# Row maxima of attention by two half-height matmuls, read as one pair of PSUM banks

## The chip, the cores and the metric

The kernel runs on one core of a Trainium2 chip. The core has five engines with queues of their own: TensorE (PE, with the weight load PEld beside it), VectorE (DVE), ScalarE (ACT), GpSimd (POOL) and SyncE (SP, which issues the DMAs). They meet through semaphores alone, and each starts its instructions in the order in which they stand in its queue. Matmul results go to PSUM, eight banks of 128 partitions x 512 float32. The metric is the device time of one execution in microseconds.

## The reference, cut to what matters

One encoder layer over 2048 tokens of width 1024. The input projection gives queries (8 heads of 64), keys and values (2 heads each) and 512 channels for a state-space model (SSM); two mixers run on them, and an output projection and a SwiGLU feed-forward follow.

```
s = einsum('bqgrd,bkgd->bgrqk', q_blk, k) * scale      # q, k: normalised and rotated
p = softmax(s, axis=-1)
o = einsum('bgrqk,bkgd->bqgrd', p, v)
```

The softmax needs no particular number as the maximum of a row: whatever is subtracted from the scores before the exponential falls out of the quotient again. It only has to lie near the true maximum.

## The kernel before

Inputs are float32. Where a product has to keep more digits than one matmul pass gives, an operand is held as a high part (rounded) and a low part (the rest).

The first stage (modulation, norm, input projection, L368) ends near 380 us. The second, 380 to 1340 us, is attention and the SSM. Attention is cut into 16 *units*: 4 blocks of 512 queries by 4 pairs of heads. For each unit `prep_q` turns the queries of two heads into operands: `qa[h]` holds the high part of head h's queries in one half of the 128 partitions and the low part in the other, `qb[h]` the high part once more and, in its second half, minus the row maxima. `ka[kv][f]` holds the high part of the keys in both halves. `prep_max` finds the maxima: for each of 4 groups of 512 keys, 2 heads and 4 blocks of 128 queries one matmul over all 128 partitions into one bank (L712, tile `ps_s1`, "ps_s" in the trace), and one VectorE maximum of it (L713, `mx`): 32 of each in a unit. The banks are `ps_1` (two) and `ps_2` (one), taken in turn. Then `m8` joins the four groups (L717), L719 turns the sign, and eight small matmuls (L723, `ps_mt`) bring the result into the rows of `qb`.

`unit` takes 16 steps of 128 keys. A step has, for each head, two matmuls into one of two `ps_st` banks (L784 with `qa` and `ka`, L785 with `qb` and `kb`, which adds minus the maximum) and an exponential on ScalarE (L787), and for both heads the product with the values (L770, `ps_o`): head 1 goes to columns 64 to 127 of TensorE's array and head 0 to columns 0 to 63, and each is two passes, since the operands are plain float32. The sums of the exponentials are on GpSimd and VectorE; `EM` says how often a step's goes to VectorE. `finish` normalises a unit (L736, L743, L749).

`advance` puts the preparation of later units between these steps, and `run(bg, 1)` the steps of the SSM: 8 chunks, with scans (L875, L876) and 1024-element products (L128, L854) on VectorE and more on GpSimd. The program order is only a priority: a scheduler with a timeline of its own decides the order in which instructions stand on each engine, and that order is fixed in the program. `tc.high_priority(KOFF)` lets the first unit's preparation come as early as its buffers allow.

Of the kernel before, what the change touches and what calls it, by code (L numbers as in the profile page):

```python
# [9 lines left out]
F32 = mybir.dt.float32  # L10
# [33 lines left out]
EM = 16  # L44
# [20 lines left out]
def tile_encoder(ctx: ExitStack, tc: tile.TileContext, I, O, stop=None, dbg=None):  # L65
# [37 lines left out]
    def rstd(pool, ss, n, width, tag):  # L103
        """(ss / width + eps) ** -0.5 on [P, n]"""
        t = pool.tile([P, n], F32, tag=tag + "a", name=tag + "a")
        GP.tensor_scalar(t, ss, 1.0 / width, EPS, op0=ALU.mult, op1=ALU.add)
        r = pool.tile([P, n], F32, tag=tag + "b", name=tag + "b")
        GP.tensor_tensor(r, t, mhalf[:, :n], op=ALU.pow)
        return r

    # ------------------------------------------------------------------ constants from parameters
# [20 lines left out]
    def cmul(ore, oim, are, aim, bre, bim, t0, t1, eng=V):  # L132
        """(ore, oim) = a * b; t0, t1 temporaries"""
# [7 lines left out]
    def rot_levels(rot, rt, lv, gs, n, eng):  # L141
        """doubles the length of the rotor tables of n groups"""
# [6 lines left out]
    with ExitStack() as p1:  # L149
# [15 lines left out]
        # ---- tables of the SSM  # L165
# [26 lines left out]
        def expand(ch, eng=V):  # L192
            """state-in, state-out and in-chunk tables of GC groups"""
# [16 lines left out]
            # re: cre*are - cim*aim; minus im: ncim*are - cre*aim  # L210
# [19 lines left out]
            # impulse responses within a chunk; columns: forward only | backward only | both  # L230
# [25 lines left out]
        # ---- conditioning vector and the columns of the small parameters  # L256
# [18 lines left out]
        def row_of(i):  # L275
            """selects row i of nr for all partitions"""
# [4 lines left out]
        def ada_chunk(c0, w, tag="ad"):  # L281
            """columns c0 to c0 + w of c_act @ w_ada"""
# [70 lines left out]
        def modulate(tf, src, ht, ks, eng):  # L353
            """hi and lo parts of the modulated rows, transposed"""
# [15 lines left out]
        def ssm_setup():  # L370
            # ---- SSM parameters
# [16 lines left out]
            # dt = exp(log_dt)  # L388
# [6 lines left out]
            # exp(lr * dt) - 1 through tanh  # L395
# [7 lines left out]
            # angle reduced to [-pi, pi]  # L403
# [30 lines left out]
            # powers 0..8  # L434
# [12 lines left out]
            # unit rotor of 8 steps (backward: conjugate) and its doublings, renormalised; decay of 8 steps  # L447
# [10 lines left out]
            # directional power tables  # L458
# [8 lines left out]
            # the state input is turned back by one chunk: pbd = pb0 * e^{-i phi}, where phi is 8 steps  # L467
            # in the direction of time; un holds e^{i phi} forward and its conjugate backward
# [7 lines left out]
        def ssm_setup2(kre, kim):  # L476
# [21 lines left out]
            # Bbar = k * b  # L498
# [7 lines left out]
        # the first tiles advance with the weights  # L506
# [20 lines left out]
        def in_main(s, ht, ta, begun):  # L527
# [8 lines left out]
            def norm_rope(src, i, n):  # L536
                """heads of src, rotated, and their reciprocal norms"""
# [50 lines left out]
        def rotors(chunks, eng, tags):  # L588
            """e^{i phi m} over the half chunks"""
# [35 lines left out]
    # ------------------------------------------------------------------ attention and SSM  # L625
# [5 lines left out]
    with ExitStack() as p2:  # L631
        ps_1 = p2.enter_context(tc.tile_pool(name="ps_1", bufs=2, space=PSUM, reuse_waits="tile"))
        ps_2 = p2.enter_context(tc.tile_pool(name="ps_2", bufs=1, space=PSUM, reuse_waits="tile"))
        ps_c = p2.enter_context(tc.tile_pool(name="ps_c", bufs=1, space=PSUM, reuse_waits="tile"))
        ps_m = p2.enter_context(tc.tile_pool(name="ps_m", bufs=1, space=PSUM, reuse_waits="tile"))
        ps_s = p2.enter_context(tc.tile_pool(name="ps_s", bufs=2, space=PSUM, reuse_waits="tile"))
# [7 lines left out]
        turn = cycle((ps_1, ps_1, ps_2))  # L644

        def scores(u, name):
            return (next(turn) if u else ps_1).tile([P, 512], F32, tag="s1", name=name)
# [14 lines left out]
        def prep_k(g, first):  # L662
            """keys as split parts: the high part of the first head, or the rest"""
            pt = scores(0, "ps_kt")
# [14 lines left out]
        def prep_q(u):  # L679
            """queries of a block for a pair of heads, as split parts"""  # L680
# [4 lines left out]
            pt = misc("ps_qt") if u else scores(u, "ps_qt")  # L685
# [9 lines left out]
            V.tensor_sub(qa[1][hi], pt[hi], qa[1][hi])  # L695
            A.copy(qa[1][lo], pt[hi])
            A.copy(qb[1][lo], qa[1][lo])
# [512 lines left out]
```

## Time and profile before

| | |
|---|---|
| median of 3 executions | 3050.98 us (3050.66 to 3051.86) |
| span of the profiled execution | 3050.2 us (the profile gives no other time of it) |
| busy PE, PEld | 2901.0 us (95%), 2129.6 us (70%) |
| busy DVE, ACT, POOL | 1598.9 us (52%), 1156.6 us (38%), 1279.9 us (42%) |
| maxima, TensorE (L712) | 512 matmuls, 211.6 us busy |
| maxima, VectorE (L713) | 512 reductions, 333.1 us busy, 682 ns each |

The span runs from the first instruction to the last. Busy shares are averages over stages that have different limits; PE's ends are modelled, so its busy time also covers gaps between close matmuls. What a change in the second stage is worth has to be read from that stage.

### The profile page before, as it was taken

The numbers are of one execution on the slowest core, as the hardware profiler recorded it, in microseconds if no ns is written. First come the engines' busy times: TensorE is split into PE (matmuls) and PEld (weight loads), VectorE is DVE, ScalarE is ACT, GpSimd is POOL, SyncE is SP. The second block draws the span as 40 slices with busy tenths as digits, with TensorE's granted clock in tenths as the row PEclk, the third lists the DMA queues.
The fourth block names the chain that finished last, engine by engine and source line by source line (L and its number), as shares of the span: only waits on it lengthen the run. The fifth ranks groups of instructions, "written<-read, shape, count | busy, mean of one in ns | idle before, by whom it ended". The sixth has DMA issues, their size and how long they took to land.

```text
span 3050.2 us, 36157 instructions
## 1 busy us (share of the span) xinstructions
PE 2901.0 (95%) x13548; PEld 2129.6 (70%) x13548; DVE 1598.9 (52%) x2271; ACT 1156.6 (38%) x2227; POOL 1279.9 (42%) x1062
## 2 busy tenths in 40 slices
PE   6998978889889999999999999999999999999998
PEld 4776835445445455458878888888888888888887
DVE  6879886777887755653343333433334332343323
ACT  3654544444444445452333222322223222232222
POOL 3647568778888977433231111211112111121112
PEclk7999998989999999999999999999999999999999
DMA  7764221111110100022254332533334332243322
GB/s 211 216 221 152 86 69 41 49 45 49 45 45 25 56 11 11 4 90 83 87 173 124 97 97 93 178 98 97 98 122 152 97 97 97 91 153 97 98 98 80
DMA packets 331648, 292.24 MB, mean 96 GB/s; under 512 B 44024, under 2 KB 278224, under 8 KB 330448
## 3 DMA queue, kind: packets, MB, share of 16 engines
q1 hardware_dynamic: 331472, 289.92, 30.0%
q8 instruction: 107, 1.75, 0.2%
q14 instruction: 69, 0.57, 0.1%
HBM read 243.24 MB, written 46.64 MB: 95 GB/s over the span
## 4 chain that ended last, share of the span: by engine, by line
PE 69%; DVE 4%; issue 1%; POOL 1%; ACT 1%; DVEq 0%; POOLq 0%; ACTq 0%
PE ps_h L1102 31%; PE ps_y L986 6%; PE ps_f L1134 5%; PE ps_f L1135 5%; PE ps_f L1136 5%; PE ps_o L770 4%; PE ps_st L784 2%; PE ps_s L712 2%; PE ps_st L785 2%; PE ps_z L986 2%; DVE xs L876 1%; DVE xs L875 1%; DVE mx L713 1%; DVE ys L128 1%; PE ps_t L977 1%
## 5 line engine op out<-in xcount | busy, mean ns | idle before, releaser
L1102 PE MATMUL ps_h<-ht,w_hi 128*128 128x512 f32 x2816 | 869.4, 390 | 2.3 <-DVE ht L1088 2.3
L1069 DVE TENSOR_TENSOR w_lo<-w_raw,w_hi 128x1024 fp32r<-128x1024 f32 x248 | 305.9, 1234 | 680.8 <-ACT w_hi L1068 680.6
L1068 ACT CAST w_hi<-w_raw 128x1024 fp32r<-128x1024 f32 x264 | 277.9, 1053 | 983.8 <-issue 628.8
L1102 PEld LDWEIGHTS ps_h<-ht,w_hi 128*128 128x128 f32 x2816 | 528.9, 188 | 112.2 <-DVE ht L1088 2.6
L1102 PE MATMUL ps_h<-ht,w_lo 128*128 128x512 f32 x1408 | 548.5, 390 | 0.4 <-DVE w_lo L1069 0.4
L1110 POOL TENSOR_TENSOR act<-th,act 128x512 fp32r<-128x512 f32 x88 | 157.1, 1786 | 775.9 <-ACT act L1109 775.9
L713 DVE TENSOR_REDUCE mx<-ps_s 128x1 f32<-128x512 f32 x512 | 333.1, 682 | 107.7 <-PE ps_s L712 105.6
L1102 PEld LDWEIGHTS ps_h<-ht,w_lo 128*128 128x128 f32 x1408 | 264.8, 188 | 55.8 <-DVE w_lo L1069 0.8
L1135 PE MATMUL ps_f<-w_hi,act 128*128 128x512 f32 x704 | 274.2, 389 | 0.0
L1136 PE MATMUL ps_f<-w_lo,act 128*128 128x512 f32 x704 | 273.9, 390 | 0.0
L1134 PE MATMUL ps_f<-w_hi,act 128*128 128x512 f32 x704 | 273.8, 390 | 0.0
L712 PE MATMUL ps_s<-ka,qa 128*128 128x512 f32 x512 | 211.6, 454 | 48.3 <-DVE mx L713 46.9
L368 PE MATMUL ps_z<-whi,ht 128*128 128x512 f32 (+1 forms) x768 | 226.9, 379 | 15.0 <-ACT ht L357 11.0
L784 PE MATMUL ps_st<-qa,ka 128*128 128x512 f32 x512 | 224.9, 439 | 14.9 <-ACT e__6941 L787 2.5
L712 PEld LDWEIGHTS ps_s<-ka,qa 128*128 128x128 f32 x512 | 93.6, 192 | 189.0 <-DVE mx L713 133.2
L785 PE MATMUL ps_st<-qb,kb 128*128 128x512 f32 x512 | 208.3, 407 | 0.1
L986 PE MATMUL ps_y<-wo,mt 128*128 128x512 f32 x768 | 186.2, 394 | 1.2 <-DVE on L751 0.9
L1108 DVE SCALAR_TENSOR_TENSOR th<-th,ps_h 128x512 f32<-128x512 f32 x88 | 60.5, 687 | 227.0 <-PE ps_h L1102 226.8
L368 PEld LDWEIGHTS ps_z<-whi,ht 128*128 128x128 f32 x768 | 141.1, 199 | 44.8 <-ACT ht L357 12.8
L784 PEld LDWEIGHTS ps_st<-qa,ka 128*128 128x128 f32 x512 | 98.9, 193 | 102.7 <-issue 21.7
L986 PEld LDWEIGHTS ps_y<-wo,mt 128*128 128x128 f32 x768 | 142.1, 188 | 35.3 <-DVE mt L980 4.7
L1135 PEld LDWEIGHTS ps_f<-w_hi,act 128*128 128x128 f32 x704 | 132.2, 188 | 27.3
(2266 smaller groups left out, 5041.5 us busy)
## 6 DMA issues: line engine op xcount, KB each, us to landing
w_raw<-in_w_ffn_in_dram SPq DMA_DIRECT2D x176, 512.0 KB
w_raw<-in_w_ffn_out_dram SPq DMA_DIRECT2D x88, 512.0 KB
wa<-in_w_ada_dram SPq DMA_DIRECT2D x48, 512.0 KB
xt<-in_x_dram SPq DMA_DIRECT2D x32, 512.0 KB
rot_d<-rot SPq DMA_DIRECT2D x16, 512.0 KB
rotl<-rot_d SPq DMA_DIRECT2D x8, 1024.0 KB
x_d<-xt SPq DMA_DIRECT2D x16, 512.0 KB
x2n<-x_d SPq DMA_DIRECT2D x16, 512.0 KB
```

What stands on the lines that cost most here:

```text
L368: T.matmul(pp[:, 0:c1 - c0], ht[:, a, k], w[:, k, c0:c1], start=k == 0 and j == 0, stop=k == KD - 1 and j == 2)
L712: T.matmul(p1_, qa[h][:, P * j:P * (j + 1)], ka[kv][f], start=True, stop=True)
L713: red = V.reduce_max(mx[:, 4 * h + j, f:f + 1], p1_, axis=AX.X)
L784: T.matmul(st_, ka[kv][k // 4][:, ks], qa[h], start=True, stop=False)
L785: T.matmul(st_, kb[kv][k // 4][:, ks], qb[h], start=False, stop=True)
L986: T.matmul(out, lhs[:, a, k], rhs[w][k][:, cs_], start=n == 0, stop=n == last)
L1068: A.copy(hi, raw)
L1069: (GP if cnt % 4 == 3 else V).tensor_sub(lo, raw, hi)
L1102: T.matmul(pp, w[:, k], ht[:, a, k], start=n == 0, stop=n == 23)
L1134: T.matmul(pf[j], act[0][:, f, js], hi[:, e], start=f == 0, stop=False)
L1135: T.matmul(pf[j], act[1][:, f, js], hi[:, e], start=False, stop=False)
L1136: T.matmul(pf[j], act[0][:, f, js], lo[:, e], start=False, stop=f == KF - 1)
```

## The change

The scores of which the maximum is taken are now made of the high parts of the queries alone, so they need only 64 partitions. Head 0's high part lies in partitions 0 to 63 and head 1's, by a changed `prep_q`, in 64 to 127 (which also saves one ScalarE copy in a unit). Two half-height matmuls (L714), one for each head, go to the two banks of one tile `pair`, and one VectorE reduction reads both (L720): 16 pairs and 16 reductions in a unit, each of twice the length. `pair` has one buffer of two banks where there were three of one; the bank left over goes to `ps_s`, which has three now, and the keys and the first unit's queries are transposed through these instead of through `ps_1`. In the first unit every second pair takes two of them too. `EM` goes from 16 to 8: in the first 13 units one more step of the 16 (the ninth) adds its two exponentials on VectorE and no longer on GpSimd.

```diff
-EM = 16
+EM = 8
-        ps_1 = ...tile_pool(name="ps_1", bufs=2, space=PSUM, ...)
-        ps_2 = ...tile_pool(name="ps_2", bufs=1, space=PSUM, ...)
+        ps_1 = ...tile_pool(name="ps_1", bufs=1, space=PSUM, ...)
-        ps_s = ...tile_pool(name="ps_s", bufs=2, space=PSUM, ...)
+        ps_s = ...tile_pool(name="ps_s", bufs=3, space=PSUM, ...)
...
-            pt = scores(0, "ps_kt")
+            pt = single("ps_kt")
...
-            V.tensor_sub(qa[1][hi], pt[hi], qa[1][hi])
-            A.copy(qa[1][lo], pt[hi])
-            A.copy(qb[1][lo], qa[1][lo])
+            V.tensor_sub(qa[1][lo], pt[hi], qa[1][hi])
+            A.copy(qb[1][lo], qa[1][hi])
...
-                for h in range(2):
-                    for j in range(4):
-                        p1_ = scores(u, "ps_s1")
-                        T.matmul(p1_, qa[h][:, P * j:P * (j + 1)], ka[kv][f], start=True, stop=True)
-                        red = V.reduce_max(mx[:, 4 * h + j, f:f + 1], p1_, axis=AX.X)
-                        yield
+                for j in range(4):
+                    js = slice(P * j, P * (j + 1))
+                    if u == 0 and j % 2:
+                        both = [single(f"ps_s{h}") for h in range(2)]
+                    else:
+                        pair = ps_1.tile([P, 2, 512], F32, tag="s1", name="ps_s1")
+                        both = [pair[:, h] for h in range(2)]
+                    for h, own in enumerate((lo, hi)):
+                        mm = T.matmul(both[h], qa[h][own, js], ka[kv][f][own], start=True, stop=True)
+                    tc.keep_in_program_order(mm)
+                    if u == 0 and j % 2:
+                        for h in range(2):
+                            red = V.reduce_max(mx[:, 4 * h + j, f:f + 1], both[h], axis=AX.X)
+                    else:
+                        red = V.reduce_max(mx[:, j::4, f], pair, axis=AX.X)
+                    yield
+                    yield
```

(`single` takes a bank of `ps_s`. The rest of the diff is comments. Lines after the maxima have numbers higher by 8: L784 is L792 now, L770 is L778, L723 is L731.)

The scheduler makes another order of it, and it differs in three ways.

First, the end of a unit on TensorE, here where the maxima of the twelfth unit become complete. Before, the last maxima stood singly between scores and value products (L770), and steps of the running unit followed them on both sides of `ps_mt`:

```order
L712 MATMUL ps_s1_9496<-ka13_4577,qa1_9265 128x512
L784 MATMUL ps_st_9930<-qa1_8784,ka12_4576 128x512
L785 MATMUL ps_st_9930<-qb1_8786,kb12_4586 128x512
L712 MATMUL ps_s1_9499<-ka13_4577,qa1_9265 128x512
L770 MATMUL ps_o_9621<-e__9919,v_sb_91 64x512
L770 MATMUL ps_o_9621<-e__9914,v_sb_91 64x512
L784 MATMUL ps_st_9939<-qa0_8783,ka13_4577 128x512
```

Now six pairs stand one behind the other at this place (the last three are shown), then the eight `ps_mt` matmuls, and then the scores of the next unit (L793), which need them:

```order
L714 MATMUL ps_s1_9093<-ka13_4574,qa0_8914 128x512
L714 MATMUL ps_s1_9093<-ka13_4574,qa1_8915 128x512
L714 MATMUL ps_s1_9097<-ka13_4574,qa0_8914 128x512
L714 MATMUL ps_s1_9097<-ka13_4574,qa1_8915 128x512
L714 MATMUL ps_s1_9115<-ka13_4574,qa0_8914 128x512
L714 MATMUL ps_s1_9115<-ka13_4574,qa1_8915 128x512
L731 MATMUL ps_mt_9122<-ident_60,mn1_4576 64x128 x4
L731 MATMUL ps_mt_9128<-ident_60,mn1_4576 64x128 x4
L793 MATMUL ps_st_9588<-qb0_8916,kb10_4581 128x512
L793 MATMUL ps_st_9622<-qb0_8916,kb10_4581 128x512
```

Ten pairs of each unit were moved into the unit's run and six behind its last value products; since `pair` has one buffer, each of the six waits for the reduction of the one ahead. This group of six stands at the end of every unit from the seventh on, and the earlier units have such groups of up to six, some with matmuls of the SSM between.

Second, the middle of a unit on TensorE. Before, a maximum's matmul stood among matmuls of its own shape, all over 128 partitions:

```order
L785 MATMUL ps_st_9895<-qb0_8785,kb12_4586 128x512
L712 MATMUL ps_s1_9453<-ka13_4577,qa0_9264 128x512
L784 MATMUL ps_st_9900<-qa1_8784,ka12_4576 128x512
L785 MATMUL ps_st_9900<-qb1_8786,kb12_4586 128x512
L770 MATMUL ps_o_9621<-e__9868,v_sb_91 64x512
```

Now a pair over 64 partitions each stands between two scores over 128:

```order
L793 MATMUL ps_st_9523<-qb0_8468,kb13_4584 128x512
L714 MATMUL ps_s1_9027<-ka11_4572,qa0_8914 128x512
L714 MATMUL ps_s1_9027<-ka11_4572,qa1_8915 128x512
L792 MATMUL ps_st_9528<-qa1_8467,ka13_4574 128x512
L793 MATMUL ps_st_9528<-qb1_8469,kb13_4584 128x512
L778 MATMUL ps_o_9238<-e__9517,v_sb_91 64x512
```

Some ten blocks of pairs in a unit stand like this, with another shape of matmul on both sides or on one.

Third, the SSM on TensorE. Its last output matmuls (`ps_y`, L895 before, L904 now) stood in the tenth unit before:

```order
L895 MATMUL ps_y_9217<-ckl_8748,ys_9035 128x128 x2
L896 MATMUL ps_y_9217<-tp_8750,ut_8804 128x128
L712 MATMUL ps_s1_8929<-ka11_4575,qa1_8784 128x512
L784 MATMUL ps_st_9378<-qa0_8304,ka01_4571 128x512
L785 MATMUL ps_st_9378<-qb0_8306,kb01_4581 128x512
```

Now they stand ahead of the maxima of the seventh unit, shortly before its `ps_mt`:

```order
L903 MATMUL ps_y_8867<-ckl_8431,ys_8687 128x128 x2
L904 MATMUL ps_y_8867<-tp_8433,ut_8484 128x128
L714 MATMUL ps_s1_6878<-ka13_4574,qa0_6662 128x512
L714 MATMUL ps_s1_6878<-ka13_4574,qa1_6663 128x512
L714 MATMUL ps_s1_6882<-ka13_4574,qa0_6662 128x512
```

So the eight chunks of the SSM lie beside six units instead of beside ten. At the start of the stage, the transposes of the keys and all maxima of the first unit stand behind the last projection matmul (L368) now; 24 of those 32 maxima stood between projection matmuls before.

## Rows read from the trace of the kernel before

**Rows 1.** Busy time in three stretches: us, PE, PEld, DVE, ACT, POOL, clock, DMA.

```profile
394.20:794.20 400.00, 343.42 (x1456) 188.00 (x1456) 306.70 (x324) 178.90 (x314) 330.22 (x222) 0.91 0.15 45
794.20:1054.70 260.50, 231.98 (x960) 125.84 (x961) 205.84 (x222) 117.52 (x209) 218.63 (x142) 0.92 0.14 40
1054.70:1284.30 229.60, 229.60 (x974) 117.03 (x972) 137.98 (x223) 119.92 (x208) 155.14 (x124) 1.00 0.03 10
```

**Rows 2.** Chain of work, 1067 to 1293 us, shares by line.

```profile
by line: PE ps_o L770 34.4%; PE ps_s L712 20.2%; PE ps_st L784 18.9%; PE ps_st L785 16.1%; PE ps_mt L723 4.0%; PE ps_rs L736 2.2%; PE ps_z L986 1.3%; PE ps_qt L687 1.0%; PE ps_ot L749 1.0%; PE ps_rt L743 0.9%; PE ps_t L977 0.2%
```

**Rows 3.** The same stretches, the maxima's reductions (L713) alone: VectorE busy, count.

```profile
394.20:794.20 400.00, 124.18 (x192) 0.91 0.15 45
794.20:1054.70 260.50, 82.84 (x128) 0.92 0.14 40
1054.70:1284.30 229.60, 104.71 (x160) 1.00 0.03 10
```

**Rows 4.** Timeline of TensorE in a late unit: start, duration, instruction.

```profile
1085.87 0.64 PE L770 MATMUL ps_o<-e__9816,v_sb 128*64 128x512 f32 x1
1085.87 0.64 PE L770 MATMUL ps_o<-e__9811,v_sb 128*64 128x512 f32 x1
...
1086.87 0.51 PE L712 MATMUL ps_s<-ka,qa 128*128 128x512 f32 x1
1087.22 0.40 PE L784 MATMUL ps_st<-qa,ka 128*128 128x512 f32 x1
```

**Rows 5.** Timeline of TensorE, a value product of one head alone.

```profile
628.98 1.07 PE L770 MATMUL ps_o<-e__6508,v_sb 128*64 128x512 f32 x2
629.98 0.50 PE L712 MATMUL ps_s<-ka,qa 128*128 128x512 f32 x1
```

**Rows 6.** Timeline of TensorE around matmuls over 64 partitions (L743, 64*128).

```profile
1069.36 0.40 PE L784 MATMUL ps_st<-qa,ka 128*128 128x512 f32 x1
1069.59 0.40 PE L785 MATMUL ps_st<-qb,kb 128*128 128x512 f32 x1
1069.92 0.46 PE L743 MATMUL ps_rt<-ident,acc 64*128 64x64 f32 x4
1070.31 0.51 PE L784 MATMUL ps_st<-qa,ka 128*128 128x512 f32 x1
1070.65 0.40 PE L785 MATMUL ps_st<-qb,kb 128*128 128x512 f32 x1
```

**Rows 7.** Timeline of VectorE in the same unit as Rows 4.

```profile
1077.23 0.69 DVE L713 TENSOR_REDUCE mx<-ps_s 128x1 f32<-128x512 f32 x1 [2.10 <-PE ps_s L712]
...
1087.42 2.08 DVE L713 TENSOR_REDUCE mx<-ps_s 128x1 f32<-128x512 f32 x3 [0.95 <-PE ps_s L712]
...
1097.81 0.19 DVE L717 TENSOR_REDUCE m<-mx 128x8 f32<-128x32 f32 x1
1098.03 0.18 DVE L719 TENSOR_SCALAR mn<-m 128x8 f32<-128x8 f32 x1
```

**Rows 8.** Timeline of TensorE where the first stage ends, the first unit's last maxima.

```profile
378.99 0.39 PE L368 MATMUL ps_z<-wlo,ht 128*128 128x512 f32 x1
...
382.04 1.10 PE L712 MATMUL ps_s<-ka,qa 128*128 128x512 f32 x2 [0.18 <-DVE mx L713]
383.32 1.10 PE L712 MATMUL ps_s<-ka,qa 128*128 128x512 f32 x2 [0.18 <-DVE mx L713]
```

**Rows 9.** Timeline of ScalarE, the first exponential.

```profile
394.16 0.60 ACT L787 ACTIVATE e__4804<-ps_st 128x512 f32<-128x512 f32 x1
```

**Rows 10.** Busy time while TensorE waited at a unit's end; columns as in Rows 1.

```profile
676.00:680.00 4.00, 0.91 (x3) 0.48 (x4) 3.97 (x2) 1.16 (x2) 4.00 (x3) 0.90 0.00 0
...
684.00:688.00 4.00, 2.67 (x7) 1.67 (x7) 3.94 (x7) 1.50 (x2) 3.73 (x6) 0.50 0.00 0
```

**Rows 11.** Two of the SSM's groups on VectorE: count, shortest/median/longest ns.

```profile
L128 DVE TENSOR_TENSOR ys<-st,st x32: 1206/2000/2364, 418.0 to 1016.6; 128x1024 f32<-128x1024 f32 x32
L875 DVE TENSOR_TENSOR_SCAN xs<-r,ys x16: 2269/3170/3371, 427.2 to 990.8; 64x1023 f32<-64x1023 f32 x16
```

More of the change, by code (lines that the diff above doesn't have):

```diff
@@ L631, in tile_encoder @@
     with ExitStack() as p2:
-        ps_1 = p2.enter_context(tc.tile_pool(name="ps_1", bufs=2, space=PSUM, reuse_waits="tile"))
-        ps_2 = p2.enter_context(tc.tile_pool(name="ps_2", bufs=1, space=PSUM, reuse_waits="tile"))
+        ps_1 = p2.enter_context(tc.tile_pool(name="ps_1", bufs=1, space=PSUM, reuse_waits="tile"))
         ps_c = p2.enter_context(tc.tile_pool(name="ps_c", bufs=1, space=PSUM, reuse_waits="tile"))
         ps_m = p2.enter_context(tc.tile_pool(name="ps_m", bufs=1, space=PSUM, reuse_waits="tile"))
-        ps_s = p2.enter_context(tc.tile_pool(name="ps_s", bufs=2, space=PSUM, reuse_waits="tile"))
+        ps_s = p2.enter_context(tc.tile_pool(name="ps_s", bufs=3, space=PSUM, reuse_waits="tile"))
         ps_o = p2.enter_context(tc.tile_pool(name="ps_o", bufs=1, space=PSUM, reuse_waits="tile"))
@@ L642, in tile_encoder, with single @@
         ab = p2.enter_context(tc.tile_pool(name="ab", bufs=3, reuse_waits="tile"))
-        turn = cycle((ps_1, ps_1, ps_2))
-        def scores(u, name):
-            return (next(turn) if u else ps_1).tile([P, 512], F32, tag="s1", name=name)
+        def single(name):
+            return ps_s.tile([P, 512], F32, tag="st", name=name)
         def misc(name, tag="am"):
@@ L684, in prep_q @@
             yield
-            pt = misc("ps_qt") if u else scores(u, "ps_qt")
+            pt = misc("ps_qt") if u else single("ps_qt")
             for j in range(4):
```

## The prediction

> **What bounds the kernel now.** I read the busy time by stretches first, because the change touches only the second stage. I cut this stage where `ps_mt` of the seventh, eleventh and sixteenth unit starts, so that the stretches hold the maxima of 6, 4 and 5 units, 192, 128 and 160 reductions [rows 3]. In the last stretch TensorE is busy all of its 229.6 us, the clock is 1.00 and VectorE has 138.0 us of work [rows 1]. The chain of waits there is nothing but TensorE's lines, and the maxima's matmuls are 20.2% of it [rows 2]. This stretch has no SSM. Work for the next stage (`ps_z` and `ps_t`) is 1.5% of the chain [rows 2], 3.4 us, so a unit takes (229.6 − 3.4) / 5 = 45.2 us.
>
> The two stretches before have the SSM beside the units, 400.0 us for six and 260.5 for four. There no engine is full: VectorE 306.7 / 400.0 = 77%, GpSimd 83%, and TensorE gets its clock for 0.91 to 0.92 on average [rows 1]. TensorE waits for reductions that stand behind the SSM's long instructions in VectorE's queue, and when it has waited long, the granted clock falls from 1.00 to 0.50, 1.2 GHz of the two levels [rows 10].
>
> **What the change is worth on TensorE alone.** A matmul of 512 columns costs 0.23 us from start to start [rows 6], so the 32 of a unit cost 7.4 us. Two matmuls in different parts of the array can run at once: the two heads' value products, in separate column halves, start in the same hundredth of a microsecond and take 1.00 us for both [rows 4], and one head alone takes the same 1.00 [rows 5]. No row shows two row halves at once. I take it that they overlap as the column halves do: 0.24 us for a pair instead of 0.47, with 0.47 as the other bound.
>
> The price is the change of shape. L743 works over 64 partitions: it starts 0.33 us after the matmul ahead, where 0.23 is usual, and the matmul behind it is followed after 0.34 [rows 6]. That is 0.10 + 0.11 = 0.21 for going in and out. It may be more, since the value product also has a long last pass ahead of the change; I take 0.30 for a block, between 0.21 and 0.40. So a lone pair costs 0.24 + 0.30 = 0.54, against 0.47 before: of the halving nothing is left. The Trainium skill (TensorEngine Tiling (Array Packing), Theoretical Speedup) gives up to twice the speed for a contraction of 64 rows or fewer; by that alone nine late units would save 9 x 16 x 0.23 = 33 us. The same page (Key Properties) says that another tiling mode drains TensorE, and with its 0.10 on either side the trace agrees with that. The sum goes by the rows.
>
> **The six pairs at a unit's end.** They are 12 matmuls in sequence on one buffer, so each waits for the reduction of the one ahead. From a maximum's matmul to its reduction pass 0.55 us (1086.87 [rows 4] to 1087.42 [rows 7]). The reduction over 1024 elements is not in the trace. It takes 0.69 us for 512 elements and 0.19 for 32 [rows 7], 1.04 ns an element, so 1.22 for 1024; the bounds are 0.69 (the second bank free) and 1.38 (twice one). I take 1.22. A waiting matmul starts some 0.03 us later, so the pitch is 0.55 + 1.22 + 0.03 = 1.8 us, and five waits take 9.0. The first unit of before shows the pattern with two buffers: two matmuls every 1.28 us, each group after a wait for a reduction [rows 8]. After the last pair follow 0.55 + 1.22, the joining (0.19) and the sign (0.18) [rows 7], with small gaps 2.2 us, until `ps_mt` starts. Before, all this lay beside value products and scores; now nothing else stands ahead of the next unit's scores on TensorE.
>
> **A late unit after the change**, then: 45.2 − 7.4 + 9 lone pairs at 0.24 (2.2) + one split pair (0.5) + ten changes of shape at 0.30 (3.0) + 9.0 + 2.2 = 54.7 us. During the six pairs TensorE works 0.24 of each 1.8 us, little like the stretch in which the clock fell [rows 10]; work at half speed around them I put at 1.3 us, between 0 and 4. That makes 56 us (53.5 to 60). Nine units look like this, since the SSM is through after six: 9 x 56 = 504 us for what took 260.5 + 229.6 = 490.1. **Term: +14 us.**
>
> **The first six units** now have all of the SSM. VectorE's work there, without maxima: 306.7 − 124.2 = 182.5 us, and from the second stretch 205.8 − 82.8 = 123.0, less four units' other work at the last stretch's (138.0 − 104.7) / 5 = 6.7, so 96 [rows 1, 3]. The maxima are 96 reductions, 117 us at 1.22 (they were 124.2); `EM` adds 12 sums of 0.69, 8 us (and takes as many from GpSimd, where they are worth nothing while it is not the last). Together 403 us. At the 77% of before this takes 523 us, without a gap 403. The denser packing should close some gaps, but each reduction has TensorE's 0.55 us ahead of it unless SSM work stands between; I take 84%, 480 us (430 to 540). **Term: 480 − 400 = +80 us.** TensorE stays just below that: 6 x 56 = 336 and, for the SSM, 343.4 + 232.0 − 10 x 45.2 = 123 [rows 1], 459 us, some of it in gaps between the pairs.
>
> **The start.** The last projection matmul is at 379.0 [rows 8] and the first exponential at 394.2 [rows 9], 15 us. Now the transposes, eight double and sixteen single reductions (8 x 1.22 + 16 x 0.64 = 20 us, 0.64 being half of 1.28 [rows 8]) and some 10 us ahead and behind stand in this gap, 30 us. The first stage gets rid of 24 maxima and 20 transposes, some 7 us. **Term: +8 us** (3 to 13).
>
> The third score bank and the saved ScalarE copy I cost at nothing: where units run without SSM, TensorE is never idle, so nothing waits for a score bank in the end. If the scores after `ps_mt` waited for ScalarE, the bank would save a part of a microsecond a unit. The last unit and the later stages have no maxima and stay.
>
> **Sum.** +8 + 80 + 14 = +102 us on a span of 3050.2, which stands 0.8 us below the median of the runs: **3153 us**.
>
> **Rivals.** *The row halves do not overlap*, so the change does not do what it says. Then a pair costs 0.23 us more; behind VectorE's work this is hidden, but in the nine late units 15 adjacent pairs each cost it: 9 x 15 x 0.23 = +31, **3184 us**. For it: no row shows two row halves at work. Against it: the column halves overlap fully [rows 4, 5]. The Trainium skill (TensorE: Matmul & The Clock Gate, Part 3) puts concurrent row tiles some 4 ns apart, which no row here can show.
>
> *The packed SSM pays for everything, and the kernel is faster.* Place: VectorE in the first six units. Its SSM instructions take 2.00 and 3.17 us in the median, but 1.21 and 2.27 at best [rows 11]. The stage has 64 of the 1024-element products and 32 scans, so at best prices 64 x 0.8 + 32 x 0.9 = 80 us less: 403 − 80 = 323, at 88% 367 us. With late units at 54.7 the sum is +8 − 33 + 2 = −23, **3028 us**. It decides once the six units take less than 400 − 8 − 14 = 378 us. For it: the trace has such instructions. Against it: GpSimd, whose work beside VectorE goes with the long ones, is 83% busy there [rows 1] and has more SSM per unit now.
>
> *The gaps stay as they were*: VectorE is no denser than 77%, and the clock falls in each group of six. 523 − 400 = 123, 9 x 59 − 490 = 41, with 8 **3222 us**. For it: the groups of maxima at the unit ends alternate with SSM work in one queue, and TensorE stalls there already.
>
> **How the numbers follow.** The forecast 0.66, gaps as before 0.14, halves in sequence 0.10, the faster case 0.07, and 0.03 for a sum that comes out at nothing. The range is 3080 to 3240. The forecast's terms at their bounds give 3 + 30 − 9 = +24 and 13 + 140 + 50 = +203; I cut both ends a little, since not all terms stand at one end together. The range holds the two slower rivals and leaves the faster case out. Within 0.2% (6 us, what a measurement here can tell from no change) is 0.02; faster 0.08, slower 0.90.
>
> **What would show it.** In the profile after, the late units' `ps_mt` should be 54 to 60 us apart, not 45, with six pairs 1.7 to 1.9 us apart ahead of each, TensorE waiting for L720; a reduction of 1.2 us; the second half of a pair within 0.02 us of the first; `ps_mt` of the seventh unit near 880 us instead of 794; the later stages shifted alone. It is wrong if the groups of six take under 5 us, or if the seventh unit's `ps_mt` comes before 790.

## The result, and the profile after

The changed kernel takes 3328.22 us (3325.25 to 3331.64, 4 runs), the kernel before 3050.82 us beside it: ratio 1.0913 (1.0897 to 1.0928). The prediction had 3153 us and a range of 3080 to 3240. The sign was right, the loss was 277 us instead of 102, well outside the range. The profiled execution has a span of 3329.9 us at a mean clock of 0.931.

I cut the stage at the first `ps_mt` matmul of the first, seventh, eleventh and last unit. In [rows 1] the first stretch began at the first exponential instead (394.2 us, now 431.3); the first `ps_mt` stood at 385.8 there. The windows view of the changed kernel (us, PE, PEld, DVE, ACT, POOL, clock, DMA) answers to [rows 1]:

```profile
423.70:979.40 555.70, 405.55 (x1680) 214.22 (x1680) 365.78 (x288) 199.84 (x349) 359.36 (x246) 0.83 0.15 42
979.40:1234.70 255.30, 211.86 (x769) 91.34 (x769) 101.84 (x111) 93.17 (x167) 129.35 (x105) 0.86 0.05 16
1234.70:1551.60 316.90, 263.97 (x965) 113.31 (x965) 135.97 (x150) 112.96 (x200) 136.99 (x110) 0.87 0.02 7
```

The last stretch matters most. Before, TensorE was busy in all of it at a clock of 1.00; now it has no SSM either, but TensorE is busy 264.0 of 316.9 us, at a clock of 0.87, and VectorE 43%. Neither engine is full. The groups on the profile page of the changed kernel (sums over the whole kernel) say why:

```profile
L720 DVE TENSOR_REDUCE mx<-ps_s 128x2 f32<-128x1024 f32 x248 | 303.6, 1224 | 328.2 <-PE ps_s L714 327.5
...
L714 PE MATMUL ps_s<-ka,qa 64*128 64x512 f32 x512 | 154.9, 569 | 168.6 <-DVE mx L720 165.2
```

The reduction waits 327.5 us for the pair and the pair 165.2 us for the reduction: the two engines take turns. In the chain of waits of the last stretch, the pairs with their reductions are over a quarter now (12.6% + 13.6%); the reduction had no share in [rows 2].

```profile
by line: PE ps_o L778 26.1%; PE ps_st L792 16.7%; DVE mx L720 13.6%; PE ps_s L714 12.6%; PE ps_st L793 11.0%; PE ps_mt L731 6.2%; issue 1.9%; PE ps_rs L744 1.6%; PE ps_qt L684 1.3%; DVE acc L783 1.2%; PE ps_ot L757 0.9%; ACT ot L738 0.9%; A
```

The timeline of TensorE shows one late unit from its `ps_mt` to the next (start, duration, instruction, idle time ahead of it):

```profile
1234.69 1.97 PE L731 MATMUL ps_mt<-ident,mn 128*64 128x128 f32 x8 [1.75 <-DVE mn L727]
1237.33 1.97 PE L731 MATMUL ps_mt<-ident,mn 128*64 128x128 f32 x8 [0.67 <-ACT qb L732]
1239.22 1.22 PE L793 MATMUL ps_st<-qb,kb 128*128 128x512 f32 x2
...
1244.02 0.50 PE L792 MATMUL ps_st<-qa,ka 128*128 128x512 f32 x1 [0.41 <-ACT e__9285 L795]
...
1249.86 0.51 PE L714 MATMUL ps_s<-ka,qa 64*128 64x512 f32 x2 [1.08 <-DVE mx L720]
...
1251.63 1.11 PE L778 MATMUL ps_o<-e__9251,v_sb 128*64 128x512 f32 x1 [0.68 <-ACT ot L738]
...
1284.36 0.50 PE L714 MATMUL ps_s<-ka,qa 64*128 64x512 f32 x2
1284.80 0.50 PE L792 MATMUL ps_st<-qa,ka 128*128 128x512 f32 x1
...
1286.65 0.50 PE L714 MATMUL ps_s<-ka,qa 64*128 64x512 f32 x2
1288.48 0.49 PE L714 MATMUL ps_s<-ka,qa 64*128 64x512 f32 x2 [1.32 <-DVE mx L720]
1290.29 0.49 PE L714 MATMUL ps_s<-ka,qa 64*128 64x512 f32 x2 [1.32 <-DVE mx L720]
...
1294.15 0.79 PE L714 MATMUL ps_s<-ka,qa 64*128 64x512 f32 x2 [1.32 <-DVE mx L720]
1296.27 0.79 PE L714 MATMUL ps_s<-ka,qa 64*128 64x512 f32 x2 [1.33 <-DVE mx L720]
1298.82 1.54 PE L731 MATMUL ps_mt<-ident,mn 128*64 128x128 f32 x6 [1.75 <-DVE mn L727]
```

Four things are to be seen. A pair occupies TensorE as long as one matmul does (x2 in 0.50 us, the second half starting 3 to 4 ns behind the first), so the row halves overlap. The six pairs stand 1.82 us apart, then 2.12, and take 12.2 us from the first to `ps_mt` (1286.65 to 1298.82). From `ps_mt` to the first score pass 4.5 us (1234.69 to 1239.22), for two groups of eight short matmul passes. And three short waits follow in the thin stretch behind it (0.41, 1.08 and 0.68 us).

The windows around the same place show the clock that goes with it:

```profile
1234.00:1238.00 4.00, 2.64 (x11) 2.24 (x12) 0.57 (x3) 0.58 (x1) 0.00 (x0) 0.50 0.00 0
...
1246.00:1250.00 4.00, 2.92 (x16) 1.41 (x16) 3.19 (x5) 1.39 (x3) 1.07 (x1) 1.00 0.00 0
1250.00:1254.00 4.00, 3.33 (x12) 1.23 (x14) 1.82 (x2) 0.95 (x2) 0.19 (x1) 0.66 0.13 39
...
1286.00:1290.00 4.00, 1.65 (x7) 0.56 (x5) 2.35 (x3) 0.00 (x0) 2.42 (x2) 1.00 0.00 0
1290.00:1294.00 4.00, 1.21 (x4) 0.40 (x4) 2.60 (x3) 0.00 (x0) 0.00 (x0) 0.78 0.00 0
1294.00:1298.00 4.00, 1.59 (x4) 0.57 (x4) 2.21 (x3) 0.00 (x0) 0.00 (x0) 0.50 0.00 0
```

During the six pairs the clock falls from 2.4 to 1.2 GHz (1.00 to 0.50), in each of the nine late units, and it is still there when the next unit's `ps_mt` and scores start. That is in line with the Trainium skill (TensorE: Matmul & The Clock Gate, HAM oscillation — how this bites in real kernels), which tells of a loop whose waits (there for DMA) bring TensorE back to half speed in every pass. In the unit shown it falls once more behind 1250 us. Four of the nine units have such a second fall and take 64.1 to 65.4 us; the other five take 62.2 to 63.3.

### The profile page after: what moved, and what is told of

It reads as the page before. It is cut to its first block, busy times and chain, and to the rows that moved or that the text cites. A ratio compares the mean times of both kernels' runs of the same rounds, so it can differ in the third digit from the quotient of the medians.

```text
span 3329.9 us, 35908 instructions
## 1 busy us (share of the span) xinstructions
PE 2982.9 (90%) x13548; PEld 2120.2 (64%) x13548; DVE 1558.2 (47%) x2049; ACT 1145.9 (34%) x2211; POOL 1199.9 (36%) x1036
## 4 chain that ended last, share of the span: by engine, by line
PE 78%; DVE 10%; POOL 5%; ACT 3%; issue 3%; DMA 2%; SPq 0%; POOLq 0%; DVEq 0%; ACTq 0%
PE ps_h L1110 29%; PE ps_o L778 7%; PE ps_y L994 5%; PE ps_f L1142 5%; PE ps_f L1144 5%; PE ps_f L1143 5%; PE ps_st L792 4%; PE ps_z L368 3%; DVE mx L720 3%; PE ps_s L714 3%; PE ps_st L793 3%; POOL acc L786 2%; PE ps_mt L731 2%; PE ps_z L994 1%; DVE rt L128 1%
## 5 line engine op out<-in xcount | busy, mean ns | idle before, releaser
L720 DVE TENSOR_REDUCE mx<-ps_s 128x2 f32<-128x1024 f32 x248 | 303.6, 1224 | 328.2 <-PE ps_s L714 327.5
L714 PE MATMUL ps_s<-ka,qa 64*128 64x512 f32 x512 | 154.9, 569 | 168.6 <-DVE mx L720 165.2
L792 PE MATMUL ps_st<-qa,ka 128*128 128x512 f32 x512 | 245.7, 481 | 10.0 <-DVE kb L671 4.4
L792 PEld LDWEIGHTS ps_st<-qa,ka 128*128 128x128 f32 x512 | 97.8, 192 | 235.8 <-issue 198.4
L368 PE MATMUL ps_z<-whi,ht 128*128 128x512 f32 (+1 forms) x768 | 226.9, 380 | 22.4 <-ACT ht L357 13.0
L714 PEld LDWEIGHTS ps_s<-ka,qa 64*128 64x128 f32 x512 | 57.7, 209 | 269.6 <-DVE mx L720 199.8
L793 PE MATMUL ps_st<-qb,kb 128*128 128x512 f32 x512 | 212.6, 422 | 0.0
L368 PEld LDWEIGHTS ps_z<-whi,ht 128*128 128x128 f32 x768 | 142.6, 202 | 52.9 <-ACT ht L357 15.2
```

Source lines behind the costliest of these rows:

```text
L368: T.matmul(pp[:, 0:c1 - c0], ht[:, a, k], w[:, k, c0:c1], start=k == 0 and j == 0, stop=k == KD - 1 and j == 2)
L714: mm = T.matmul(both[h], qa[h][own, js], ka[kv][f][own], start=True, stop=True)
L720: red = V.reduce_max(mx[:, j::4, f], pair, axis=AX.X)
L792: T.matmul(st_, ka[kv][k // 4][:, ks], qa[h], start=True, stop=False)
L793: T.matmul(st_, kb[kv][k // 4][:, ks], qb[h], start=False, stop=True)
```

## The experiments

One table for all of them. The marks are the starts of the first `ps_mt` of a unit in the TensorE timeline of the profiled execution: of the first unit, from there to the seventh, from the seventh to the last, and from the last to the end of the span. "Late" is the mean distance over the last four units, which have no SSM in any kernel here. The code cuts below are shortened, with constants put in for names.

| kernel | median us | ratio to before | first | to 7th | 7th to last | to end | late |
|---|---|---|---|---|---|---|---|
| before | 3050.82 | | 385.8 | 408.4 | 490.1 | 1765.9 | 46.1 |
| changed | 3328.22 | 1.0913 (1.0897–1.0928) | 423.7 | 555.8 | 572.2 | 1778.3 | 63.2 |
| e1 full height | 3337.89 | 1.0942 (1.0926–1.0959) | 421.3 | 555.7 | 585.1 | 1773.5 | 65.0 |
| e2 two pairs | 3150.76 | 1.0334 (1.0318–1.0349) | 410.7 | 392.5 | 578.7 | 1766.7 | 46.9 |
| e3 half-height singles | 3125.01 | 1.0249 (1.0232–1.0266) | 394.3 | 428.7 | 529.6 | 1766.8 | 51.4 |
| e4 EM 16 | 3320.37 | 1.0883 (1.0867–1.0900) | 425.5 | 547.2 | 570.4 | 1774.9 | 63.2 |
| e5 spread late | 3242.71 | 1.0629 (1.0612–1.0647) | 423.3 | 555.5 | 484.0 | 1780.9 | 53.2 |
| e6 start | 3304.89 | 1.0832 (1.0815–1.0848) | 398.8 | 557.2 | 568.0 | 1773.5 | 63.2 |
| e7 bank move | 3163.43 | 1.0374 (1.0356–1.0393) | 382.6 | 469.7 | 536.1 | 1773.2 | 54.7 |
| e8 spread, start | 3195.96 | 1.0479 (1.0463–1.0495) | 401.0 | 506.6 | 510.6 | 1775.1 | 53.7 |
| e9 before, no SSM | 2871.98 | 0.9420 (0.9401–0.9439) | 410.0 | 275.0 | 410.4 | 1775.2 | 46.1 |
| e10 changed, no SSM | 3128.25 | 1.0260 (1.0240–1.0281) | 405.3 | 379.7 | 562.9 | 1777.3 | 62.5 |
| e11 two pairs, full height | 3151.18 | 1.0336 (1.0320–1.0351) | 409.5 | 394.9 | 574.2 | 1767.7 | 45.8 |
| e12 kept busy | 3288.37 | 1.0786 (1.0768–1.0804) | 425.0 | 472.0 | 617.5 | 1772.1 | 59.4 |

The theory after the result was *one buffer*: `pair` has a single buffer, so the pairs gather at a unit's end, the engines take turns there, and the clock falls. The rival was *shapes*: the changes between half and full height cost far more than the 0.30 us that I gave them.

**e1: full height, all else as changed.**

```diff
-T.matmul(both[h], qa[h][own, js], ka[kv][f][own], start=True, stop=True)
+T.matmul(both[h], qa[h][:, js], ka[kv][f], start=True, stop=True)
```

> The changed kernel with its pairs at full height: both maxima matmuls of a pair work over all 128 rows (so the maxima are of high plus low parts again), and there is no change of shape around them. Bank, single buffer, 1024-element reduction and instruction order stay those of the changed kernel (twelve matmuls in a row at each unit's end). Theory one buffer (the pair tile has one buffer, so TensorE and VectorE take turns, the pairs gather at the end of a unit, and the clock falls there): the time stays, 3300 to 3345 us, late ps_mt still 61 to 64 us apart. Rival shapes (the many changes between half and full height drain TensorE far beyond the 0.30 us I priced): most of the loss goes, under 3200 us, late ps_mt under 53 us apart.

Without any change of shape around the maxima the kernel is no faster; the late units are even 1.8 us longer, a little over what was expected. The shapes are not what costs.

**e2: two buffers for the pair.**

```diff
-ps_1 ... bufs=1        ps_s ... bufs=3        ps_c ... bufs=1
+ps_1 ... bufs=2        ps_s ... bufs=2        (SSM uses the bank of ps_m)
```

> The changed kernel with two buffers for the pair tile (four banks). The two banks come from the third score bank and from the SSM's bank: the SSM now shares the bank of the small transposes. Half height and 1024-element reductions stay. In the order, the twelve matmuls at the unit's end are gone; a late unit has 16 blocks of maxima between scores and value products, and ps_mt stands ahead of the last value products again. Theory one buffer: late ps_mt 48 to 51 us apart, no fall of the clock between them, the whole 3110 to 3200 us (the first six units may pay for the shared bank). Rival shapes: 16 blocks instead of 12, late ps_mt stay 60 us or more apart, the whole 3290 or more.

The late units come back to 46.9 us with all 16 pairs at half height, even under the 48 to 51 expected. In the windows view of e2 TensorE is busy all the time again, at full clock:

```profile
1194.30:1381.90 187.60, 186.53 (x775) 79.88 (x773) 109.84 (x123) 92.30 (x161) 108.82 (x87) 1.00 0.03 9
```

That the whole is 100 us over the kernel before lies in two other places: 25 us at the start (first `ps_mt` at 410.7 for 385.8), and 69 in the stretch with the SSM, which reaches into the eleventh unit here (784 us from the first to the twelfth `ps_mt`, 714 before). The SSM shares a bank with the small transposes in this version; that this is the reason is likely, but no run shows it. So this version shows the cause in the late units and is no way out.

**e3: the kernel before with half-height matmuls in its own three banks.**

```diff
-for h in range(2):
-    for j in range(4):
-        p1_ = scores(u, "ps_s1")
-        T.matmul(p1_, qa[h][:, P * j:P * (j + 1)], ka[kv][f], ...)
+for j in range(4):
+    both = [scores(u, "ps_s1") for h in range(2)]
+    for h, own in enumerate((lo, hi)):
+        T.matmul(both[h], qa[h][own, P * j:P * (j + 1)], ka[kv][f][own], ...)
```

> The kernel before with only the half-height matmuls: maxima from the high parts, heads alternating, in its own three single banks with 512-element reductions; one ScalarE copy less per unit. In the order a late unit has 25 blocks of maxima, mostly a single half each, so there are about 50 changes of shape and little overlap. Theory one buffer: only the shapes cost, 25 blocks at 0.24 + 0.30 us less 7.4 us of full matmuls give about 51 us between late ps_mt, the whole 3090 to 3140 us. Rival shapes: twice the changes of the changed kernel, late ps_mt over 60 us apart, the whole over 3250.

Both numbers came as *one buffer* had them. 25 blocks cost 51.4 − 46.1 + 7.4 = 12.7 us, 0.51 each, for the 0.54 that I had worked out from the neighbouring rows. This prices the half-height matmul with its changes of shape, without any wait: TensorE is never idle in the last four units.

**e4: the changed kernel with EM = 16.**

> The changed kernel with EM back at 16, so that twelve sums in the first six units go back from VectorE to GpSimd; in the order of a late unit nearly nothing moves. Theory one buffer: VectorE waits for pairs a good part of its time there, so the sums fall mostly into its gaps: 3315 to 3328 us. A third theory, that VectorE is simply over-full in the first six units since EM loads it: 8 us of sums and the stalls behind them, 20 us or more, under 3308 us.

3320 us: `EM` is worth some 8 us of the 277, most of it in the first six units (547.2 for 555.8).

**e5: the pairs of late units tied to places between scores, still one buffer.** A dependency that only orders TensorE's queue ties 16 pairs to 26 places:

```diff
+for i, p_ in enumerate(pairs.get(u + 1, ()) if u >= 6 else ()):
+    if 26 * i // 16 == 2 * k + h:
+        tc.add_manual_dep(sc.ins, p_.ins.name, <order only>)
```

> The changed kernel, still with one buffer for the pair, but from the seventh unit on each pair of the next unit is tied in TensorE's order to a place between this unit's scores (16 pairs over 26 places), so that no more than two matmuls of maxima stand together and ps_mt again has scores on both sides. Theory place in the order (one buffer is enough as long as other work stands between two pairs; it is the twelve matmuls in a row at the unit's end that cost): late ps_mt 46 to 50 us apart from the eighth unit on, granted clock near 1.00, the first six units as in the changed kernel, the whole 3190 to 3225 us. Rival turns (with one buffer every pair waits for a reduction, wherever it stands): late ps_mt 56 us or more apart, the whole over 3260 us.

It fell between the theories: 53.2 us, not 46 to 50 and not 56. The lump itself is worth 63.2 − 53.2 = 10.0 us a unit, with the clock back at 0.98 in the same seven units:

```profile
1089.40:1462.70 373.30, 334.34 (x1349) 144.34 (x1348) 196.21 (x201) 158.23 (x281) 208.16 (x166) 0.98 0.03 9
```

TensorE is idle 39 us of these 373, 5.6 a unit. The waits view of e5 says that the pairs wait for reductions only 9.5 us in all; a little more is for the query operands (`qa`), which this placing asks for early, and most of the rest for exponentials, one short wait at a time:

```profile
PE ps_s L717 <- DVE mx L724: 9.5, 27, 1.1
PE ps_s L717 <- ACT qa L694: 5.8, 7, 0.8
PE ps_s L717 <- ACT qa L690: 4.7, 7, 0.7
```

So waiting for the one buffer costs 1.4 us a unit once pairs stand apart. Of the 17.1 us that a late unit loses (63.2 for 46.1), the lump is 10.0, and the scheduler builds it where the maxima have fewer buffers (e7 below) and not where the pair has two (e2).

**e6: the first unit's preparation in the pair's banks** instead of the score banks (transposes take one half of a pair tile, all its maxima are pairs).

> The changed kernel, but the first unit's preparation takes all its space from the pair's two banks instead of the score banks: transposes of keys and queries use one half of a pair tile, and all 16 pairs of the first unit are pairs. In the order 20 of its 32 maxima and most transposes then stand ahead of the last projection matmul again, where the changed kernel has none. Theory banks (the start was late because the score banks come free only with the first stage's end): first ps_mt at 392 to 402 us instead of 423.7, the whole 22 to 32 us shorter, 3298 to 3310. Rival VectorE (the reductions and the SSM's first chunk fill VectorE there either way): first ps_mt after 415, the whole over 3318.

As the first theory had it: `ps_mt` at 398.8 and 23 us gained. In the timeline of e6 maxima stand between the first stage's projections again:

```profile
376.26 0.49 PE L714 MATMUL ps_s<-ka,qa 64*128 64x512 f32 x2
376.69 0.73 PE L368 MATMUL ps_z<-whi,ht 128*128 128x512 f32 x2
...
381.78 0.49 PE L714 MATMUL ps_s<-ka,qa 64*128 64x512 f32 x2
383.59 0.50 PE L714 MATMUL ps_s<-ka,qa 64*128 64x512 f32 x2 [1.32 <-DVE mx L720]
...
398.84 1.64 PE L731 MATMUL ps_mt<-ident,mn 128*64 128x128 f32 x8
```

**e7: the kernel before with the bank moved and nothing else.**

```diff
-turn = cycle((ps_1, ps_1, ps_2))      ps_s ... bufs=2
+turn = cycle((ps_1,))                 ps_s ... bufs=3
```

> The kernel before with only the bank moved: two single banks for the maxima instead of three, three for the scores; full-height matmuls and 512-element reductions stay. In the order a late unit now ends with six matmuls of maxima in a row and eight matmuls of ps_mt, where before nothing of the kind stood. Theory place in the order: late ps_mt 51 to 56 us apart with waits for L713 at the unit's end and a fall of the clock, the whole 3110 to 3200 us. Rival (what costs is that two banks are read in one go; two single banks alternate well enough): late ps_mt under 47 us apart, the whole within 25 us of before.

This one edit, with neither half height nor pairs, costs 3.7%, some 113 us of the 277. A late unit takes 54.7 us, and its end in the timeline of e7 is the changed kernel's in small, two matmuls a turn instead of a pair:

```profile
1275.57 1.10 PE L711 MATMUL ps_s<-ka,qa 128*128 128x512 f32 x2 [0.55 <-DVE mx L712]
1276.86 1.09 PE L711 MATMUL ps_s<-ka,qa 128*128 128x512 f32 x2 [0.19 <-DVE mx L712]
1279.27 1.94 PE L722 MATMUL ps_mt<-ident,mn 128*64 128x128 f32 x8 [1.31 <-DVE mn L718]
1281.87 1.54 PE L722 MATMUL ps_mt<-ident,mn 128*64 128x128 f32 x6 [0.67 <-ACT qb L723]
```

**e8: e6, and the pairs of all units tied as in e5.**

> The changed kernel with both: the first unit's preparation in the pair's banks, and the pairs of every unit, those beside the SSM too, tied to places between the scores. Theory place in the order: late ps_mt 46 to 50 us apart, first ps_mt near 397, and in the first six units TensorE no longer waits in groups at the unit's end, so that half of their loss or more is gone: 3080 to 3140 us. Rival VectorE over-full (the first six units are long since VectorE has the whole SSM there, not since the pairs wait): their ps_mt stay 88 us or more apart, the whole 3155 to 3190 us.

3196 us, above what either theory expected. The first six units lose 49 of their extra 147 us (506.6, or 84 us a unit): less than half, and more than the rival allowed. The SSM then reaches into the seventh, and placing by hand does no better in late units than in e5 (53.7 us).

**e9 and e10: both kernels without the SSM** in the second stage; its result is a constant.

> The kernel before without the SSM's eight chunks in the second stage (their result is filled with a constant); everything else stays. Without it every unit should look like its late ones: ps_mt 45 to 46 us apart from the first to the last, 15 units in some 682 us instead of 898.5, the whole 2820 to 2850 us.

> The changed kernel without the SSM's eight chunks (left out as in the kernel before without them). Theory unit's end (each unit loses the same 18 us in its lump of pairs and behind it, early or late, and the SSM beside the units costs no more than before): ps_mt 62 to 65 us apart from the first unit on, the whole 3130 to 3160 us, some 310 above the kernel before without the SSM. Rival VectorE over-full (in the first six units it is the SSM packed on VectorE that costs, 147 us more than before): without the SSM only the late units' loss and what belongs to the start remain in proportion, the early units 50 us or less apart, the whole under 3040 us.

The two answer the question that was open, why the first six units lost so much. Windows of e9, from the first to the seventh `ps_mt` and on to the last:

```profile
410.00:685.00 275.00, 268.95 (x1108) 135.70 (x1108) 155.39 (x244) 141.75 (x245) 199.19 (x159) 0.99 0.04 10
685.00:1095.40 410.40, 410.40 (x1743) 209.96 (x1741) 235.75 (x382) 213.88 (x371) 292.48 (x233) 1.00 0.04 11
```

and the same of e10:

```profile
405.30:785.00 379.70, 310.86 (x1129) 131.97 (x1128) 146.50 (x152) 135.50 (x238) 193.66 (x156) 0.86 0.03 7
785.00:1347.90 562.90, 468.56 (x1729) 202.12 (x1729) 233.77 (x254) 203.08 (x360) 266.00 (x214) 0.87 0.03 8
```

Units without SSM are 45.7 us apart before and 62.8 after, early or late: 17.1 a unit, 257 for fifteen (942.6 − 685.4). That is all of the difference between e9 and e10 (256 us). The totals missed: e10 came out 2 us under its range and e9 22 us above, because its first `ps_mt` is at 410 and not 386 and its end 9 us longer, and that also takes the start out of the difference, which I had put at 310. In e9's trace none of the first unit's 32 maxima stands ahead of the last projection matmul (371.8 us), where 24 did before; why the scheduler orders it so was not pursued.

**e11: e2 at full height.**

> The changed kernel with two buffers for the pair (SSM on the bank of the small transposes) and full-height matmuls, so no change of shape around the maxima; a late unit has the same kind of order as with half height, 16 places of maxima. Theory halving pays nothing (a lone pair costs 0.24 + 0.30 us at half height and 0.47 at full): late ps_mt 45 to 46 us apart, about 1 us less than at half height, the whole within 15 us of it, 3135 to 3155. Rival (the halves do save TensorE time): late ps_mt 49 us or more apart, the whole 3165 or more.

The same time as e2 within 0.5 us, and 45.8 us a late unit for 46.9, about what was expected. Halving the maxima on TensorE is worth nothing here, or 1.1 us less than nothing, as worked out: 16 lone pairs at 0.54 less 7.4 us of full matmuls are 1.2.

**e12: TensorE kept busy in the lump.** Same order; full matmuls into the SSM's bank, four behind each of the pairs 11 to 15 of a unit and eight behind the last:

```diff
+if u >= 7 and 4 * f + j >= 10:
+    fill = misc("fill", "sm")
+    for n in range(8 if 4 * f + j == 15 else 4):
+        T.matmul(fill, ka[kv][0][:, 0:P], qa[0], start=True, stop=True)
```

> The changed kernel, one buffer, same order; from the eighth unit on four full matmuls into the SSM's bank that nothing reads stand behind each of the last five pairs but one of a unit's end, and eight behind the last, so that TensorE works on while it waits there. They only add work; a waiting pair comes some 0.2 us later at most. Theory clock (of the 18 us a late unit loses, some 7 are work at half the clock during and after the lump): granted clock near 1.00 there, late ps_mt 55 to 59 us apart instead of 63, the whole 3270 to 3300 us. Rival waits alone (the clock falls where TensorE has little to do anyway): late ps_mt 62 us or more apart, the whole 3315 or more.

The total is not to be compared, since the SSM shares its bank with the added matmuls and moved to later units. The late units are: the pitch of the pairs stays 1.82 us, and in the windows of e12 the clock stays at 1.00, in the lump (second row) and in the thin stretch behind `ps_mt` (first row):

```profile
1348.00:1352.00 4.00, 2.95 (x18) 1.33 (x18) 2.48 (x4) 1.11 (x3) 1.27 (x1) 1.00 0.02 4
...
1388.00:1392.00 4.00, 3.62 (x16) 2.03 (x15) 2.74 (x3) 0.00 (x0) 0.00 (x0) 1.00 0.00 0
```

A late unit takes 59.4 instead of 63.2 us, just outside the 55 to 59 expected. The added matmuls hold nothing up: from the last pair to `ps_mt` pass 2.5 us with and without them. So the clock is worth 3.8 us a unit, between the 7 of the theory and nothing.

No version with the SSM beat the kernel before; the nearest is e3 at 3125 us. The late units of e2 and e11, 46.9 and 45.8 us for 46.1, show that halves gain nothing there.

## Why the prediction was wrong in size

From the marks, the loss is +37.9 (start) + 147.4 (first six units) + 82.1 (nine late units) + 12.4 (after the last `ps_mt`) = 279.8 us of span. The prediction had 8 + 80 + 14 + 0.

**What held.** The row halves overlap, the reduction takes 1.22 us, the pairs at a unit's end stand 1.82 us apart, and the whole lump takes 12.2 us where 0.24 + 9.0 + 2.2 = 11.4 were priced. The change of shape eats the halving (e3, e11). The rivals *row halves do not overlap* and *packed SSM pays* are out, though the second had something true in it: see below.

**The first six units** were the step that failed: +147 for +80. I took VectorE's work and divided it by a density of 84%, with TensorE's as a second sum that stayed below. VectorE had less work than the 403 us that I priced, 365.8, and yet took 555.7 us: it is busy 66%, and TensorE 73%. With one buffer the two do not run beside each other at a unit's end, so neither's work bounds the time. The evidence is TensorE's waits for the reductions, and for the sign behind the last of them (`mn`), which grew from 37.7 to 122.5 us. VectorE in turn waits 83.3 us for pairs. Over these six units TensorE's waits were, before (us, times, longest):

```profile
PE ps_s L712 <- DVE mx L713: 30.0, 13, 7.5
PE ps_mt L723 <- DVE mn L719: 7.7, 2, 5.3
```

and are now:

```profile
PE ps_s L714 <- DVE mx L720: 99.4, 31, 10.7
PE ps_mt L731 <- DVE mn L727: 23.1, 2, 16.7
```

The lump is lost there as in late units, which e10 shows: six units without SSM take 379.7 us, 104.7 more than in e9. The SSM then adds 555.8 − 379.7 = 176 us. Over the whole stage its eight chunks add 1127.9 − 942.6 = 185 us, where before they added 898.5 − 685.4 = 213. So the packed SSM was 28 us cheaper; how much of that lies in the gaps of the lump no run tells. The right sum was 15 units at +17.1, less 28. The rival that the gaps stay as they were came nearest, with 3222 us, but by the same step: it divided VectorE's work by 77%.

**The late unit** was mis-sized: 63.2 us for 56, and the step was the lump's surroundings, not the lump. Half clock was put at 1.3 us and is 3.8 (e12). From `ps_mt` to the scores I added nothing to what it took before, 0.97 us for each of the two groups of eight, with scores between:

```profile
1145.23 1.04 PE L723 MATMUL ps_mt<-ident,mn 128*64 128x128 f32 x8
1146.20 0.50 PE L784 MATMUL ps_st<-qa,ka 128*128 128x512 f32 x1
...
1148.24 1.04 PE L723 MATMUL ps_mt<-ident,mn 128*64 128x128 f32 x8
```

It takes 4.5 us now, since the second eight wait 0.67 us for ScalarE's copy and all run at half speed. In e12, at full clock, it takes 2.8 (1336.21 to 1338.98), so 1.8 of these 2.6 us are in the 3.8. The three short waits in the thin stretch are 2.2 us more in the unit shown. Some 2 of the 7.2 us are left that no run took apart. The 45.2 us from which I started came out by luck: the `ps_z` matmuls of [rows 2] that I took off the stretch all stand behind its end (1285.86 us and later). Its first three units are in fact 45.2 to 45.3 us apart, but the last two are 46.1 and 47.9; why was not pursued.

**The start** was mis-sized: +38 for +8. I had priced the reductions and not what stands with them in the gap ahead of `ps_mt`: eight subtractions for `kb` (5.6 us) and the SSM's first chunk (10.1). And the first stage, which I had made 7 us shorter, ends only 0.8 sooner (last projection matmul at 378.17 for 378.99). VectorE is full in the gap (window 400 to 424 of the changed kernel):

```profile
400.00:424.00 24.00, 10.31 (x41) 5.60 (x40) 23.61 (x26) 6.79 (x12) 4.91 (x4) 0.67 0.06 22
```

e6 gives back 25 of the 38 us by the banks alone; the other 13 stay open.

**The last unit and what follows** I left at nothing, as if they only shifted; it is +12.4. Before, 24 matmuls of the next stage (`ps_z`) stood beside the last unit, behind its `ps_mt`:

```profile
1287.66 2.79 PE L986 MATMUL ps_z<-wg,yt 128*128 128x512 f32 x11
...
1309.81 2.79 PE L986 MATMUL ps_z<-wg,yt 128*128 128x512 f32 x11
```

Now the first of them stand behind the unit's last value product, where TensorE has little else:

```profile
1606.91 5.49 PE L994 MATMUL ps_z<-wg,yt 128*128 128x512 f32 x12 [3.23 <-DVE on L759]
```

From the last `ps_mt` to the last value product it is 41.5 us for 54.2, so the unit itself has not become longer. From there to the first `ps_y` matmul of the next stage it is 27.9 us for 11.8 (TensorE is busy in 12.3 of them), and that stage's `ps_y` matmuls take 9.4 us more, with the other `ps_z` among them. The table bears it out: the four kernels that keep the 24 beside the last unit (before, e2, e3, e11) end 1766 to 1768 us after the last `ps_mt`, and all others, which have none there, 1772 to 1781. e9 is one of these and has no lump. What makes the scheduler move them no run shows.

**What was not in the prediction:** that moving one bank does a good part of this by itself. e7 costs 113 of the 277 us with two single buffers instead of three, and 8.6 of the 17.1 in a late unit. I looked at the pairs and took the third score bank to be the harmless part, "at nothing"; what mattered was the buffer that it took away. The Trainium skill (TensorEngine Tiling (Array Packing), Theoretical Speedup) promises up to twice the speed for 64 rows. The pair alone agrees with that (two matmuls in 0.50 us), but in a unit's time e11 against e2 shows none of it.

## What to carry to other kernels

Before a PSUM bank is taken from one use to another, look at what the scheduler makes of the use that loses it: with fewer buffers the same matmuls can end up in a lump at a point where nothing else is ready, and then two engines take turns at a clock that falls. Price such a lump for every pass of the loop, also where another engine seems to be the bound, and price what follows it at half clock. A half-height matmul between full-height ones gained nothing here; whether it does in larger groups no run tried.

## What the runs showed of the hardware

Two things I had not expected. A thin stretch does not always bring the clock down: behind `ps_mt`, 2.95 us of work in 4 kept 1.00 in e12, while in the changed kernel 2.92 in 4 (1246 to 1250) was followed by 0.66. The lump ahead, kept busy in the one and idle in the other, does not decide it alone: behind the same idle lump five of the nine late units of the changed kernel kept 1.00 in their thin stretch, as the one after the unit shown:

```profile
1310.00:1314.00 4.00, 3.64 (x17) 1.44 (x16) 3.31 (x5) 1.61 (x3) 0.53 (x1) 1.00 0.01 4
```

What does decide it stays open. And the fall reaches the pairs themselves: at 0.50 their pitch grows from 1.82 to 2.12 us, although TensorE does only one pair in it.
